# Modulation slices asked for only while the projections' loader has nothing waiting

## The chip, the core and the metric

The kernel runs on one core of one Trainium2 chip. The metric is the device time of one launch in microseconds (us), the median of several runs. TensorE is called PE (its weight loads PEld), VectorE DVE, ScalarE ACT, GpSimd POOL, SyncE SP. SP issues most of the DMAs.

## The reference

Two decoder layers work on x, 1024 tokens by 1024 features in float32. In each layer three vectors, shift, scale and gate, come from the conditioning vector c and modulate the layer's input and output:

```python
mod = c_act @ w_mod + b_mod                    # c_act = silu(c), w_mod: 1024 x 3072 per layer
shift, scale, gate = jnp.split(mod[:, None, :], 3, axis=-1)
h = rms_norm(x, pre_gain) * (1.0 + scale) + shift
proj = h @ w_in                                # 1024 x 3088
...                                            # attention, retention, gated linear attention
y = jnp.concatenate([a_out, r_out, g_out], axis=-1) @ w_out
return x + gate * rms_norm(y, post_gain)
```

Shift and scale are needed before a layer's projections, gate only at its output.

## The kernel before

The program is written out by Python generators. PE's instructions stand in the order in which the generators emit them; the other engines' order is made by a scheduler that starts from that order. The main thread of `layer(l)` goes through the projections: gg and rg (gates), then rq, rk and rv with the retention of eight token tiles, then gqk, gv and kv, then aq0 and aq1, ag0 and ag1, and the output product with w_out. All products are done as three passes over a high and a low part of each operand, so every weight is split when it is loaded.

Beside the main thread run jobs: generators that do one step and yield a delay. A planner's clock, `clk` (in us), advances with an estimated cost for each matmul (`mult`); `pump` runs each job whose due time has passed. The delays stand in the table `L` by name (`lat`), with "@1" for layer 1.

Two kinds of jobs bring in weights, and both use the same five stage buffers, `stage()`, of 128 x 512 floats (tag "st", BST = 5), which other rows use too (the row of post-norm gain, L378).

- The loader of the projections' weights. `request` puts a quarter of a unit (256 KB) into the list `queue` and starts the job `loader` if none runs. `loader` takes an entry, issues its DMA on SP (L152) and appends it to `flying`; when more than LAG + 1 = 3 would be in flight it converts the oldest first (`convert`). A conversion writes the high part (ACT L147 or DVE L149) and the low part (DVE or POOL L535) into the unit's place in the arena, and frees the stage buffer. Between two steps it yields 1.2.
- The modulation, `mod_third(l, j)` with j = 0 for shift, 1 for scale, 2 for gate. For each half of 512 columns it takes eight slices of w_mod, 128 x 512 floats each (256 KB): stage buffer, DMA on SP, and one product-and-sum on DVE into `acc` (L363 for the first, L365 for the others), and yields `mod2`, 4.0. After the eighth it yields `mod3`, and matmuls sum `acc` over its partitions (one of 128 x 512 with a matrix of ones for the gate, four with a single column otherwise). Layer 0's shift and scale are made by another function at the start.

Layer l starts the job for its own gate after its gg and rg projections, and behind it the next layer's scale and shift. There are 64 such slices: 16 each for gate 0, scale 1, shift 1 and gate 1.

Other lines that are spoken of: L163 all matmuls, L178 transposes; in the retention, ACT's L147 copies the transposed q and k out of PSUM, DVE's L1173 masks the scores, L1192 and L1194 renew the running state stR; L963 writes the low part of a gated output, which SP stores to mixS; POOL's L638 is a power for the norms. L147 is thus both a weight's conversion (arena<-st) and a copy out of PSUM (t<-aux, t<-mm).

Of the kernel before, what the change touches and what calls it, by code (L numbers as in the profile page):

```python
# [91 lines left out]
def trunk(ctx: ExitStack, tc: tile.TileContext, ins, cst, out):  # L92
# [24 lines left out]
    def stage():  # L117
        return gp.tile([P, 512], F32, tag="st", name=nm("st"), bufs=BST)
# [7 lines left out]
    def aux(dt=F32):  # L126
        return ps.tile([P, 512], dt, tag="aux", name=nm("aux"), bufs=8 - MMB)
# [23 lines left out]
    def dma(k, dst, src):  # L151
        {"S": nc.sync, "A": A, "P": G}[EN[k]].dma_start(dst, src)  # L152
# [9 lines left out]
    def mult(dst, lhsT, rhs, start, stop, cost=None):  # L162
        T.matmul(dst, lhsT, rhs, start=start, stop=stop)  # L163
        if cost is not None:
            clk[0] += cost
            return
        n = 1
        for d in rhs.shape[1:]:
            n *= d
        c = n / 2400.0  # L170
        if rhs.dtype == F32R:
            c = max(c, 0.107 if lhsT.shape[-1] > 64 else 0.055)
        else:
            c = max(4 * c, 0.21 if n > 2 else 0.03)
        clk[0] += c
# [5 lines left out]
    def lat(key, l):  # L181

        return L[key + "@1"] if l and key + "@1" in L else L[key]

# [3 lines left out]
    def flag(name, lat=0.0):  # L188
        flags[name] = clk[0] + lat
# [73 lines left out]

    modc = {}
    modg = {}

    def mod_rows(l, j, eng=nc.sync):
        rows = t1()[0:16, 0:P]
        eng.dma_start(rows[0:8, :], b_mod[l:l + 1, j * D:(j + 1) * D].rearrange("o (k p) -> (o k) p", p=P))
        eng.dma_start(rows[8:16, :], pre_g[l:l + 1, :].rearrange("o (k p) -> (o k) p", p=P))  # L270
        return rows

    def mod_rows_t(rows, pool=aux):
        pr = pool()
# [68 lines left out]
    def mod_third(l, j):  # L343
        wv = w_mod[l].rearrange("(p k) n -> p k n", k=KT)
        if j < 2:
            mod_tile(l, j)
            rows = mod_rows(l, j)
            yield lat("mod1", l)
            rc = mod_rows_t(rows)
        else:  # L350
            res = cp.tile([P, D], F32, name=nm("modg"), tag="modg")
            modg[l] = res
        for hh in range(2):
            c0 = j * D + 512 * hh
            acc = gp.tile([P, 512], F32, tag="acc", name=nm("acc"), bufs=1)
            if j == 2:
                G.memset(acc, 0.0)
                nc.sync.dma_start(acc[0:1, :], b_mod[l:l + 1, c0:c0 + 512])
            for k in range(KT):
                wt = stage()  # L360
                dma("lwm", wt, wv[:, k, c0:c0 + 512])
                if k == 0 and j < 2:
                    V.tensor_scalar(acc, wt, c_act[:, k:k + 1], None, ALU.mult)  # L363
                else:
                    V.scalar_tensor_tensor(acc, wt, c_act[:, k:k + 1], acc, ALU.mult, ALU.add)  # L365
                yield lat("mod2", l)
            yield lat("mod3", l)
            pm = aux()
            if j < 2:
                for b in range(4):  # L370
                    mult(pm[:, b:b + 1], acc[:, b * P:(b + 1) * P], ones[:, 0:1], True, True)
                mod_cols(l, j, hh, pm, rc)
                if j == 0:
                    flag(("modh", l, hh), lat("mod4", l))
            else:
                mult(pm, allones, acc, True, True)
                gain = stage()
# [87 lines left out]
    def unit(l, name):  # L465
        return place(PLACE[l][name])


    queue, flying = [], []

    def convert():
        conv, st = flying.pop(0)
# [123 lines left out]
    def sw_second():  # L596
        drain()
        for k in range(4):
# [7 lines left out]
            sw_split("T4", k, s4, "t4")  # L606
            yield L["sw1"]
        for name in ("T2", "T3", "T4"):
# [48 lines left out]
    def pre(l, t, xt, early=False, soon=False):  # L657
# [1010 lines left out]

B2, B1, BS, BST, MMB, SMB = 10, 8, 11, 5, 3, 3
EN = {"shw0": "V", "shw1": "A", "shw2": "A", "shw3": "A", "slw0": "V", "slw1": "G", "slw2": "V", "slw3": "G", "sht2": "A", "sht3": "A", "sht4": "A", "slt2": "V", "slt3": "G", "slt4": "G", "sd": "V", "mh0": "A", "mh1": "A", "mh2": "A", "mh3": "A", "mf": "A", "ms0": "V", "ms1": "V", "ms2": "V", "ms3": "V", "yg0": "V", "yg1": "V", "ml0": "V", "ml1": "V", "ml2": "V", "ml3": "V", "mod0": "A", "mod1": "V", "qst": "S", "smh": "S", "sml": "S", "sm0": "S", "sm1": "S", "lao": "S", "sao": "S", "lmix": "S", "ssg": "S", "lsg": "S", "ssr": "S", "lsr": "S", "lx": "S", "sx": "A", "lw": "S", "lwm": "S", "whi0": "V", "whi1": "A", "whi2": "A", "whi3": "A", "wlo0": "V", "wlo1": "V", "wlo2": "V", "wlo3": "G", "xn0": "V", "xn1": "V", "hlo0": "V", "hlo1": "V", "rot0": "V", "rot1": "V", "rdec": "V", "kslo": "V", "qslo": "V", "vlo": "G", "kT": "A", "qT": "A", "sprev": "A", "pn": "G", "pf0": "A", "aoc": "A", "hng": "V", "mh": "A", "gso": "V", "mg": "V", "mgl": "V", "rT": "A", "rv": "A", "gv": "A", "gk": "A", "ak0": "V", "ak1": "V", "ak2": "V", "ak3": "V", "kd0": "G", "kd1": "G", "kd2": "G", "kx1": "G", "kx2": "G", "kx3": "V", "kx4": "V", "qb": "G", "stx": "V"}  # L1670
L = {"sw1": 0.4, "ld1": 1.2, "ld2": 1.2, "ld1@1": 1.2, "ld2@1": 1.27, "swW00": 0.0, "swT1": 0.0, "swW11": 0.4, "swW10": 0.5, "tt1": 8.0, "tt2": 1.75, "tb1": 24.5, "tb2": 0.75, "pf3": 13.2, "pf1": 6.35, "pf2": 4.16, "mod1": 4.6, "mod2": 4.0, "mod3": 13.29, "mod4": 7.04, "mod5": 3.36, "mod6": 9.04, "pre1": 7.44, "kv1": 3.1, "kv2": 2.11, "aq1": 6.0, "aq7": 6.0, "ag1": 5.44, "aq2": 2.4, "aq6": 5.2, "aq3": 10.21, "aq4": 7.36, "aq5": 3.6, "hn1": 8.93, "hn2": 2.85, "gz1": 11.18, "gz2": 8.13, "gl1": 2.76, "gd3": 15.9, "gc1": 0.62, "gc2": 1.94, "gc3": 1.33, "gc4": 0.87, "gc6": 0.86, "gc5": 1.14, "rc1": 0.8, "rc2": 1.09, "rc3": 5.87, "rc4": 2.51, "fin1": 7.28, "lay1": 1.13, "gc4@1": 0.93, "mod2@1": 4.0, "mod3@1": 15.1, "mod5@1": 3.36, "mod6@1": 4.11, "pre1@1": 7.44, "kv1@1": 2.79, "kv2@1": 5.28, "aq1@1": 4.8, "aq7@1": 5.28, "ag1@1": 6.25, "aq2@1": 0.82, "aq6@1": 6.0, "aq3@1": 10.9, "aq4@1": 4.4, "aq5@1": 5.15, "hn1@1": 8.12, "hn2@1": 2.85, "gz1@1": 15.91, "gz2@1": 10.94, "gl1@1": 4.6, "gd3@1": 15.9, "gc1@1": 0.48, "gc2@1": 1.94, "gc3@1": 1.33, "gc6@1": 0.86, "gc5@1": 1.04, "rc1@1": 0.37, "rc2@1": 0.84, "rc3@1": 1.9, "rc4@1": 2.79, "fin1@1": 4.28, "lay1@1": 1.7}
CHUNK = 7
LAG = 2
VDB = 8
# [32 lines left out]
```

## Time and profile before

| | us |
|---|---|
| three runs | 1005.52, 1007.46 (median), 1011.33 |
| the profiled execution | 1010.63 |
| its span in the trace | 1008.9 |
| PE busy | 975.4 |
| DVE busy | 684.5 |
| ACT busy | 408.8 |
| POOL busy | 234.4 |

How to read the rows. In a table by stretch a row has the stretch, its length, then the busy time of PE, PEld, DVE, ACT and POOL with the number of instructions, then the granted clock of PE (1.00 is full), the busy share of the 16 DMA engines and GB/s. In a timeline a row has the start, the time taken, the engine, line, operation, written and read tiles and shapes, how many instructions are merged, and in brackets the idle time before with what ended it; SPq is a DMA's issue, not its transfer. A row of the chain of waits has start, time and what; a DMA there lasts from its issue to its landing. In the DMA list the last figures are the size of one and the median from issue to landing. A row of the waits has total, number of times and the longest.

### The profile page before, as it was taken

How to read it: one execution, taken by the hardware profiler on the slowest of the kernel's cores; microseconds unless marked ns; L12 is line 12 of the kernel's file. 1: busy time of each engine (PE TensorE's matmuls, PEld its weight loads, DVE VectorE, ACT ScalarE, POOL GpSimd, SP SyncE). 2: the span in 40 equal slices, each digit the busy share in tenths (PEclk: the TensorE clock that was granted, in tenths of full speed). 3: DMA queues.
4: the chain of work that ended last, by engine and by line, in shares of the span. 5: the costliest groups of instructions: out<-in, count | busy, mean ns of one | idle time of the engine just before them, and what ended most of it. 6: DMA issues, size and time to landing. Idle time of an engine off the chain costs nothing.

```text
span 1008.9 us, 19610 instructions
## 1 busy us (share of the span) xinstructions
PE 975.4 (97%) x7137; PEld 829.5 (82%) x7137; DVE 684.5 (68%) x1680; ACT 408.8 (41%) x1152; POOL 234.4 (23%) x275
## 2 busy tenths in 40 slices
PE   5899999899999999999999999999999999999897
PEld 1499999888998777778889999998899877777785
DVE  3789857757666778564578275785666577566876
ACT  2476311223322656632465232123332256663321
POOL 2310001223320234330112000113332034544100
PEclk8899999999999999999999999999999999999999
DMA  9942513623326355577655251353132434378883
GB/s 293 308 137 76 173 45 100 170 81 96 96 74 199 89 149 163 171 239 244 214 157 173 64 158 32 108 150 100 41 104 85 125 90 130 112 236 249 265 263 140
DMA packets 129836, 148.73 MB, mean 147 GB/s; under 512 B 14046, under 2 KB 94152, under 8 KB 129740
## 3 DMA queue, kind: packets, MB, share of 16 engines
q1 hardware_dynamic: 124044, 137.92, 45.3%
q10 hardware_dynamic: 5696, 9.56, 2.6%
q8 instruction: 56, 0.92, 0.4%
q14 instruction: 40, 0.33, 0.1%
HBM read 109.17 MB, written 36.18 MB: 144 GB/s over the span
## 4 chain that ended last, share of the span: by engine, by line
PE 80%; DVE 8%; DMA 7%; issue 2%; POOL 1%; ACT 1%; SPq 0%; POOLq 0%; DVEq 0%; ACTq 0%
PE mm L163 61%; PE aux L163 14%; PE aux L178 5%; DMA st<-in_w_in_dram 2%; DMA st<-in_w_out_dram 1%; POOL sm L638 1%; DMA xk<-in_x_dram 1%; DMA wm<-in_w_mod_dram 1%; DMA t<-aoS 1%; DVE arena L535 1%; DMA st<-in_w_mod_dram 1%; DMA t<-sgS 1%; DVE t L328 0%; DVE st L572 0%; DMA mixF<-t 0%
## 5 line engine op out<-in xcount | busy, mean ns | idle before, releaser
L163 PE MATMUL mm<-arena 128*128 128x256 f32 (+2 forms) x1824 | 299.2, 318 | 1.8 <-ACT arena L707 1.8
L163 PE MATMUL mm<-arena,arena 128*128 128x256 f32 (+2 forms) x1824 | 300.7, 318 | 0.0
L163 PEld LDWEIGHTS mm<-arena 128*128 128x128 f32 x1824 | 254.6, 191 | 26.5 <-issue 4.1
L163 PEld LDWEIGHTS mm<-arena,arena 128*128 128x128 f32 x1824 | 254.1, 189 | 25.5 <-issue 4.6
L638 POOL TENSOR_TENSOR sm<-sm,mhalf 128x1 f32<-128x1 f32 (+1 forms) x64 | 56.1, 877 | 347.0 <-DVE sm L637 328.6
L163 PE MATMUL mm<-arena,mx 128*128 128x512 f32 (+1 forms) x564 | 132.4, 392 | 2.9 <-ACT kept L1335 2.9
L163 PEld LDWEIGHTS mm<-arena,mx 128*128 128x128 f32 x564 | 103.1, 191 | 27.1 <-ACT kept L1335 3.3
L147 ACT ACTIVATE t<-aux 128x256 f32<-128x256 f32 (+2 forms) x124 | 55.7, 467 | 76.1 <-PE aux L178 64.8
L147 ACT ACTIVATE arena<-st 128x512 fp32r<-128x512 f32 x94 | 56.1, 626 | 59.1 <-DMA st<-in_w_in_dram 21.4
L535 POOL TENSOR_TENSOR arena<-st,arena 128x512 fp32r<-128x512 f32 x31 | 43.2, 1395 | 138.9 <-ACT arena L147 100.9
L926 POOL TENSOR_TENSOR smx<-smx,sm 128x512 f32<-128x512 f32 x32 | 36.1, 1127 | 124.3 <-DVE sm L925 116.1
L535 DVE TENSOR_TENSOR arena<-st,arena 128x512 fp32r<-128x512 f32 x77 | 59.5, 795 | 6.1 <-ACT arena L147 4.1
L922 ACT ACTIVATE smx<-smx,sm 128x129 f32<-128x129 f32 x128 | 49.9, 392 | 28.4 <-DVE sm L919 28.4
L178 PE MATMUL aux<-c_ident,t 128*128 128x128 f32 (+1 forms) x292 | 48.8, 285 | 7.6 <-DVE t L669 7.2
L365 DVE SCALAR_TENSOR_TENSOR acc<-st,c_act,acc 128x512 f32<-128x512 f32 x60 | 45.5, 759 | 12.6 <-DMA st<-in_w_mod_dram 12.1
L178 PEld LDWEIGHTS aux<-c_ident,t 128*128 128x128 f32 (+1 forms) x292 | 35.4, 145 | 15.2 <-DVE t L669 9.0
L701 ACT ACTIVATE t<-aux,mod,mod 128x128 f32<-128x128 f32 x68 | 25.9, 458 | 43.8 <-DVE t L1242 18.2
L970 ACT ACTIVATE t<-aux 128x256 f32<-128x256 f32 x32 | 12.3, 383 | 75.5 <-PE aux L163 63.4
L163 PEld LDWEIGHTS aux<-t,mx 32*128 32x128 f32 (+1 forms) x896 | 39.5, 187 | 3.8 <-issue 2.1
L163 PE MATMUL aux<-t,mx 32*128 32x32 f32 (+1 forms) x896 | 40.7, 273 | 0.0
L917 DVE COPY_PREDICATED smx<-c_curmask,aux 128x256 f32<-128x256 int32 x64 | 25.5, 447 | 18.8 <-ACT smx L147 15.3
L1242 DVE SCALAR_TENSOR_TENSOR t<-t,sm,t 128x512 f32<-128x512 f32 x32 | 24.0, 779 | 18.6 <-DMA t<-in_x_dram 11.9
(220 smaller groups left out, 1384.3 us busy)
## 6 DMA issues: line engine op xcount, KB each, us to landing
st<-in_w_in_dram SPq DMA_DIRECT2D x96, 256.0 KB, 3.1
st<-in_w_mod_dram SPq DMA_DIRECT2D x64, 256.0 KB, 3.3
st<-in_w_out_dram SPq DMA_DIRECT2D x52, 256.0 KB, 3.8
mx<-mixS SPq DMA_DIRECT2D x20, 512.0 KB, 6.2
mixS<-t SPq DMA_DIRECT2D x72, 128.0 KB, 2.3
wm<-in_w_mod_dram SPq DMA_DIRECT2D x12, 512.0 KB, 8.0
t<-in_x_dram SPq DMA_DIRECT2D x24, 256.0 KB, 4.8
t<-tabS SPq DMA_DIRECT2D x16, 256.0 KB, 3.7
```

The costliest lines, as they stand in the source:

```text
L147: A.activation(dst, src, AF.Copy)
L163: T.matmul(dst, lhsT, rhs, start=start, stop=stop)
L178: T.transpose(dst, src, idn)
L365: V.scalar_tensor_tensor(acc, wt, c_act[:, k:k + 1], acc, ALU.mult, ALU.add)
L535: e.tensor_tensor(lo, st, f(hi), ALU.subtract)
L638: G.tensor_tensor(r, r, mhalf[:, :w], ALU.pow)
L701: A.activation(hf[:, ks], at[kt], AF.Identity, scale=gain, bias=shift)
L917: V.copy_predicated(sv, curmask.unsqueeze(1).to_broadcast((P, 2, P)), pv[:, :, n // P - 1, :])
L922: A.activation(sm[:, h, :], sm[:, h, :], AF.Exp, bias=mx[:, h:h + 1], accum_out=sums[:, h:h + 1])
L926: eng("pn").tensor_tensor(sm[:, :, 0:128], sm[:, :, 0:128], rs.unsqueeze(2).to_broadcast((P, 4, P)), ALU.mult)
L970: A.activation(sq, po, AF.Square)
L1242: V.scalar_tensor_tensor(xt[j], yg[j], r, xt[j], ALU.mult, ALU.add)
```

## The change

Before each slice of the modulation the job now looks whether the loader has anything in `queue` or in `flying`, and as long as it has, yields `mod7`, 1.0, and looks again. The delay after each slice, `mod2`, goes from 4.0 to 2.0 in both layers. The two lists are created earlier in the file, which moves line numbers by one to three. The tests are made while the program is written out, against the planner's clock; the program on the chip contains no such test.

```diff
     modc = {}
     modg = {}
+    queue, flying = [], []
...
             for k in range(KT):
+                while queue or flying:
+                    yield lat("mod7", l)
                 wt = stage()
                 dma("lwm", wt, wv[:, k, c0:c0 + 512])
                 if k == 0 and j < 2:
...
-    queue, flying = [], []
-
     def convert():
...
-L = {... "mod1": 4.6, "mod2": 4.0, ... "mod2@1": 4.0, ...}
+L = {... "mod1": 4.6, "mod7": 1.0, "mod2": 2.0, ... "mod2@1": 2.0, ...}
```

More of the change, by code (lines that the diff above doesn't have):

```diff
@@ L1670 @@
 EN = {"shw0": "V", "shw1": "A", "shw2": "A", "shw3": "A", "slw0": "V", "slw1": "G", "slw2": "V", "slw3": "G", "sht2": "A", "sht3": "A", "sht4": "A", "slt2": "V", "slt3": "G", "slt4": "G", "sd": "V", "mh0": "A", "mh1": "A", "mh2": "A", "mh3": "A", "mf": "A", "ms0": "V", "ms1": "V", "ms2": "V", "ms3": "V", "yg0": "V", "yg1": "V", "ml0": "V", "ml1": "V", "ml2": "V", "ml3": "V", "mod0": "A", "mod1": "V", "qst": "S", "smh": "S", "sml": "S", "sm0": "S", "sm1": "S", "lao": "S", "sao": "S", "lmix": "S", "ssg": "S", "lsg": "S", "ssr": "S", "lsr": "S", "lx": "S", "sx": "A", "lw": "S", "lwm": "S", "whi0": "V", "whi1": "A", "whi2": "A", "whi3": "A", "wlo0": "V", "wlo1": "V", "wlo2": "V", "wlo3": "G", "xn0": "V", "xn1": "V", "hlo0": "V", "hlo1": "V", "rot0": "V", "rot1": "V", "rdec": "V", "kslo": "V", "qslo": "V", "vlo": "G", "kT": "A", "qT": "A", "sprev": "A", "pn": "G", "pf0": "A", "aoc": "A", "hng": "V", "mh": "A", "gso": "V", "mg": "V", "mgl": "V", "rT": "A", "rv": "A", "gv": "A", "gk": "A", "ak0": "V", "ak1": "V", "ak2": "V", "ak3": "V", "kd0": "G", "kd1": "G", "kd2": "G", "kx1": "G", "kx2": "G", "kx3": "V", "kx4": "V", "qb": "G", "stx": "V"}
-L = {"sw1": 0.4, "ld1": 1.2, "ld2": 1.2, "ld1@1": 1.2, "ld2@1": 1.27, "swW00": 0.0, "swT1": 0.0, "swW11": 0.4, "swW10": 0.5, "tt1": 8.0, "tt2": 1.75, "tb1": 24.5, "tb2": 0.75, "pf3": 13.2, "pf1": 6.35, "pf2": 4.16, "mod1": 4.6, "mod2": 4.0, "mod3": 13.29, "mod4": 7.04, "mod5": 3.36, "mod6": 9.04, "pre1": 7.44, "kv1": 3.1, "kv2": 2.11, "aq1": 6.0, "aq7": 6.0, "ag1": 5.44, "aq2": 2.4, "aq6": 5.2, "aq3": 10.21, "aq4": 7.36, "aq5": 3.6, "hn1": 8.93, "hn2": 2.85, "gz1": 11.18, "gz2": 8.13, "gl1": 2.76, "gd3": 15.9, "gc1": 0.62, "gc2": 1.94, "gc3": 1.33, "gc4": 0.87, "gc6": 0.86, "gc5": 1.14, "rc1": 0.8, "rc2": 1.09, "rc3": 5.87, "rc4": 2.51, "fin1": 7.28, "lay1": 1.13, "gc4@1": 0.93, "mod2@1": 4.0, "mod3@1": 15.1, "mod5@1": 3.36, "mod6@1": 4.11, "pre1@1": 7.44, "kv1@1": 2.79, "kv2@1": 5.28, "aq1@1": 4.8, "aq7@1": 5.28, "ag1@1": 6.25, "aq2@1": 0.82, "aq6@1": 6.0, "aq3@1": 10.9, "aq4@1": 4.4, "aq5@1": 5.15, "hn1@1": 8.12, "hn2@1": 2.85, "gz1@1": 15.91, "gz2@1": 10.94, "gl1@1": 4.6, "gd3@1": 15.9, "gc1@1": 0.48, "gc2@1": 1.94, "gc3@1": 1.33, "gc6@1": 0.86, "gc5@1": 1.04, "rc1@1": 0.37, "rc2@1": 0.84, "rc3@1": 1.9, "rc4@1": 2.79, "fin1@1": 4.28, "lay1@1": 1.7}
@@ new lines @@
+L = {"sw1": 0.4, "ld1": 1.2, "ld2": 1.2, "ld1@1": 1.2, "ld2@1": 1.27, "swW00": 0.0, "swT1": 0.0, "swW11": 0.4, "swW10": 0.5, "tt1": 8.0, "tt2": 1.75, "tb1": 24.5, "tb2": 0.75, "pf3": 13.2, "pf1": 6.35, "pf2": 4.16, "mod1": 4.6, "mod7": 1.0, "mod2": 2.0, "mod3": 13.29, "mod4": 7.04, "mod5": 3.36, "mod6": 9.04, "pre1": 7.44, "kv1": 3.1, "kv2": 2.11, "aq1": 6.0, "aq7": 6.0, "ag1": 5.44, "aq2": 2.4, "aq6": 5.2, "aq3": 10.21, "aq4": 7.36, "aq5": 3.6, "hn1": 8.93, "hn2": 2.85, "gz1": 11.18, "gz2": 8.13, "gl1": 2.76, "gd3": 15.9, "gc1": 0.62, "gc2": 1.94, "gc3": 1.33, "gc4": 0.87, "gc6": 0.86, "gc5": 1.14, "rc1": 0.8, "rc2": 1.09, "rc3": 5.87, "rc4": 2.51, "fin1": 7.28, "lay1": 1.13, "gc4@1": 0.93, "mod2@1": 2.0, "mod3@1": 15.1, "mod5@1": 3.36, "mod6@1": 4.11, "pre1@1": 7.44, "kv1@1": 2.79, "kv2@1": 5.28, "aq1@1": 4.8, "aq7@1": 5.28, "ag1@1": 6.25, "aq2@1": 0.82, "aq6@1": 6.0, "aq3@1": 10.9, "aq4@1": 4.4, "aq5@1": 5.15, "hn1@1": 8.12, "hn2@1": 2.85, "gz1@1": 15.91, "gz2@1": 10.94, "gl1@1": 4.6, "gd3@1": 15.9, "gc1@1": 0.48, "gc2@1": 1.94, "gc3@1": 1.33, "gc6@1": 0.86, "gc5@1": 1.04, "rc1@1": 0.37, "rc2@1": 0.84, "rc3@1": 1.9, "rc4@1": 2.79, "fin1@1": 4.28, "lay1@1": 1.7}
```

## The prediction, made before the changed kernel ran

> **What bounds the kernel now.** I read the engine shares first, then a table of busy time by stretch, then the PE timeline in the stretches that are not full, and last the queue of each engine that PE waited for there. Lines are those of the kernel before.
>
> ```profile
> span 1008.9 us, 19610 instructions
> PE 975.4 (97%) x7137; PEld 829.5 (82%) x7137; DVE 684.5 (68%) x1680; ACT 408.8 (41%) x1152; POOL 234.4 (23%) x275
> ...
> 150.00:175.00 25.00, 24.46 (x203) 23.25 (x203) 16.78 (x51) 3.50 (x8) 2.96 (x3) 1.00 0.35 98
> 175.00:200.00 25.00, 21.91 (x176) 20.73 (x176) 19.06 (x51) 8.51 (x17) 6.66 (x5) 0.98 0.57 160
> 200.00:225.00 25.00, 25.00 (x141) 21.69 (x140) 13.88 (x35) 5.60 (x13) 6.98 (x10) 0.89 0.26 77
> 225.00:675.00 450.00, 449.39 (x3410) 390.32 (x3410) 304.50 (x762) 184.51 (x535) 99.87 (x119) 1.00 0.47 142
> 675.00:690.00 15.00, 12.34 (x75) 10.21 (x75) 7.27 (x19) 4.08 (x9) 3.30 (x3) 1.00 0.64 185
> 690.00:900.00 210.00, 209.88 (x1747) 172.50 (x1746) 138.25 (x354) 99.57 (x323) 70.56 (x84) 1.00 0.37 110
> ```
>
> PE is the bound: its first figure nearly equals the length of the stretch. The change moves no work into the start or the last 100 us, so between 150 and 900 us only PE's idle time can be won: 0.54 + 3.09 + 0 + 0.61 + 2.66 + 0.12 = 7.0 us, and what the granted clock of 0.98 and 0.89 (the figure before the last two) costs. Where it is lost:
>
> ```profile
> 172.48 0.71 PE L163 MATMUL aux<-t 64*128 64x128 f32 x6 [0.54 <-DVE t L963]
> ...
> 194.43 2.11 PE L163 MATMUL mm<-arena,arena 128*128 128x512 f32 x8
> 199.62 1.23 PE L163 MATMUL aux<-t 64*128 64x128 f32 x8 [3.09 <-ACT t L147]
> 200.78 3.78 PE L163 MATMUL mm<-arena,arena 128*128 128x512 f32 x8
> ...
> 209.60 0.38 PE L163 MATMUL aux<-stR,t 128*128 128x128 f32 x2
> ```
>
> ```profile
> 195.50:198.90 3.40, 1.04 (x5) 0.51 (x3) 0.35 (x1) 0.71 (x2) 0.01 (x1) 1.00 0.86 252
> 198.90:202.30 3.40, 2.67 (x12) 2.17 (x13) 1.18 (x3) 0.67 (x2) 1.25 (x1) 0.50 0.80 229
> 202.30:205.70 3.40, 3.40 (x13) 2.92 (x12) 0.00 (x0) 0.00 (x0) 0.00 (x0) 0.50 0.37 120
> ...
> 678.00:681.40 3.40, 2.12 (x21) 1.82 (x20) 1.43 (x3) 1.11 (x2) 0.00 (x0) 1.00 0.96 318
> ```
>
> The 3.09 us stall costs more than itself: the 3.4 us around it hold 1.04 us of matmul (31%), and the next 6.8 us run at clock 0.50. A stretch with 2.12 of 3.40 (62%) kept 1.00. I call 195 to 210 us place A and 675 to 690 us place B. Both are the last tiles of a layer's retention stage, where layer 0's or 1's weight slices gqk, gv and kv come through the five stage buffers.
>
> ```profile
> 192.08 0.63 ACT L147 ACTIVATE arena<-st 128x512 fp32r<-128x512 f32 x1 [1.23 <-DMA st<-in_w_in_dram]
> 194.41 0.63 ACT L147 ACTIVATE arena<-st 128x512 fp32r<-128x512 f32 x1 [1.70 <-DMA st<-in_w_in_dram]
> 194.95 0.36 ACT L147 ACTIVATE t<-mm 128x256 f32<-128x256 f32 x1
> 198.19 0.63 ACT L147 ACTIVATE arena<-st 128x512 fp32r<-128x512 f32 x1 [2.87 <-DMA st<-in_w_in_dram]
> ```
>
> ```profile
> 186.84 4.86 SPq L152 DMA_DIRECT2D st<-in_w_in_dram  x3
> 191.80 0.41 SPq L152 DMA_DIRECT2D mixS<-t  x1
> 192.30 0.38 SPq L152 DMA_DIRECT2D st<-in_w_in_dram  x1
> ...
> 194.00 2.20 SPq L152 DMA_DIRECT2D st<-in_w_mod_dram  x3
> ```
>
> ```profile
> 165.96 5.29 DMA st<-in_w_mod_dram
> ...
> 192.30 5.80 DMA st<-in_w_in_dram
> ```
>
> These are ACT's row, SP's issues and two pieces of the chain of waits. ACT takes its list in order. The conversion of kv's last slice sits at 198.19, because that slice, asked for at 192.30, needed 5.80 us; the copy that PE needs stands behind it. At 172.48 it is a slice of the modulation that blocks: asked for at 165.96, 5.29 us.
>
> **The change part by part.** The counts on every engine are the same in both programs (6197 PE, 1682 DVE, 1004 ACT, 280 POOL, 638 SP); it moves instructions only. Each slice moved is one DMA on SP and one product on DVE; the sum over bias and gain, one matmul per half of the gate, moves with it. Compared in program order, the conversions of the projection weights keep their places within some 50 matmuls; what changes is which load stands in front of which.
>
> *At 172.* The sixth slice of the gate's second half, which blocked DVE there, is now asked for before gqk's loads instead of between them:
>
> ```profile
> 171.34 0.75 DVE L365 SCALAR_TENSOR_TENSOR acc<-st,c_act,acc 128x512 f32<-128x512 f32 x1 [3.83 <-DMA st<-in_w_mod_dram]
> ```
>
> The eight products still stand ahead of the same L963, but no load of theirs is now asked for behind a load of gqk. Gain 0.54 (bounds 0 and 0.54).
>
> *Place A.* Order of requests before: gqk, slice, gqk, gqk, gv, slice, gv, gv, slice, gv, kv x4, gain row, slices. After: all slices of the gate, gqk x4, gv x3, gain row, gv, kv x4, slices. The buffers then free like this:
>
> ```profile
> 187.66 1.29 POOL L535 TENSOR_TENSOR arena<-st,arena 128x512 fp32r<-128x512 f32 x1
> ...
> 190.62 1.89 DVE L535 TENSOR_TENSOR arena<-st,arena 128x512 fp32r<-128x512 f32 x3
> ```
>
> kv's first load now takes the buffer of gv's last slice (free at 187.66 + 1.29 = 188.95, 2.1 later than now), the others those freed by the three products of 0.63 each, the first of them moved ahead of one instruction (L1151): 190.6, 191.6, 192.2. So kv's last load is asked for at 192.2, as before; only the store of mixS at 191.80 no longer stands before it, and no row of gain right behind it. What it takes from there is the open term. The page's median for such a load is 3.1 us, this one took 5.80:
>
> ```profile
> st<-in_w_in_dram SPq DMA_DIRECT2D x96, 256.0 KB, 3.1
> st<-in_w_mod_dram SPq DMA_DIRECT2D x64, 256.0 KB, 3.3
> ```
>
> Three loads stand within 1.6 us ahead of it, so I take 4.0: landing at 196.2 (bounds 195.3 and 198.0). From the landing (198.10) to PE's start (199.62) are now 1.5; one copy more (0.36, the row at 194.95) stands between, so PE starts again at 198.1. PE itself runs out at 194.43 + 2.11 = 196.54, and the gate's product is moved in front of that:
>
> ```profile
> L163 PE MATMUL aux<-acc,c_ones x8: 591/592/593, 153.5 to 702.3; 128*128 128x512 f32 x8
> ```
>
> so 197.1. The stall is 1.0 instead of 3.09; the 3.4 us around it hold 2.4 us of matmul (70%, above the 62% that kept the clock), so the half clock goes. From 199.62 to 209.60 PE now needs 9.98, of which 6.08 at half clock; without it 6.94. *What is late next:* eight slices now follow kv in a row, 2 units of the planner's clock apart instead of 4, and three of their products stand on DVE right before the update of stR, for which PE waits at 209.60. Behind the store that follows ACT's copy, they are asked for at about 198.8, 199.2 and 199.6; 3.3 us to land and 0.75 of product give 204.4, and stR is renewed 1.3 us later, at 205.7. PE would be there at 198.1 + 6.94 = 205.0, so it waits 0.7 and stands at that matmul at 205.7 instead of 209.60. With the 0.59 of the moved product, which falls away later, the gain is 4.5. Bounds: 0, if the load takes 5.8 again, and 3.09 + 3.04 = 6.1 with no stall and no half clock. [...]
>
> *Place B.* The same, without the clock:
>
> ```profile
> 680.77 0.72 PE L163 MATMUL aux<-t 64*128 64x128 f32 x8 [1.28 <-ACT t L147]
> 681.41 3.04 PE L163 MATMUL mm<-arena 128*128 128x512 f32 x12
> 685.46 0.46 PE L163 MATMUL aux<-stR,t 128*128 128x128 f32 x2 [1.01 <-DVE stR L1194]
> ```
>
> ```profile
> 679.60 0.63 ACT L147 ACTIVATE arena<-st 128x512 fp32r<-128x512 f32 x1 [3.77 <-DMA st<-in_w_in_dram]
> 680.14 0.58 ACT L147 ACTIVATE t<-aux 128x512 f32<-128x512 f32 x1
> 681.71 1.40 ACT L147 ACTIVATE arena<-st 128x512 fp32r<-128x512 f32 x2 [0.99 <-DMA st<-in_w_in_dram]
> ```
>
> kv's loads are asked for 5 us (first) to 1 us (last) earlier, since two slices no longer stand in between. But in the changed order ACT has two more conversions, those of kv's last two slices, in front of the copy at 680.14; they wait for landings that now come at 681.71 and, two conversions in 1.40 us, about 682.5. 1 us earlier, the last is converted at 682.1, the copy done at 682.7 and PE's matmul of 680.77 comes 2 us later. Behind it 1.01 of wait, 0.4 of a second one and the product moved ahead (0.59) fall away. I take 0; bounds a gain of 2.66 (all idle time there) and a loss of 5.4 (the slow rival below).
>
> *Elsewhere.* Between 270 and 285 three slices go through one buffer one after another, and DVE waits for them, up to 2 us by an estimate from their 3.3 us to land. PE covers it: in the 450 us from 225 on it idled 0.61 us, though DVE waited in the same manner there (nine waits of all, 12.1 us):
>
> ```profile
> DVE acc L365 <- DMA st<-in_w_mod_dram: 12.1, 9, 3.8
> ```
>
> 0 taken, 1 us lost if that cover fails. The added waiting step issues nothing on any engine, it only delays the planner's job; nothing hangs on it but the sums of gate, gain and shift, which layer 1 needs from 525 us on and which stand no later in the new order than in the old.
>
> **Sum.** -0.5 - 4.5 + 0 = -5.0 us against the profiled execution, which took 1010.63 (span 1008.9 and 1.73 around it). The median of the three runs, 1007.46, is 3.2 lower, and the runs spread by 5.8; a stall that sets off the half clock in one run and not in the next would spread them so. So I count 4.0 of the 5.0 for the median: **1003.5 us**.
>
> **Rivals.** *The load stays late* (A unchanged, kv's last load 5.8 us again): landing 198.0, PE at 199.9, stall 2.8, half clock stays; -0.5 in all, 1007. For it: kv's last load is asked for no earlier. Against: fewer transfers around it. [...]
>
> *Slower: place B becomes what A was.* If kv's last load lands there at 682.5 as now, since the row of gain is asked for ahead of three of kv's loads instead of behind them, the copy behind it is done at 683.7 and PE's matmul comes at 683.8 instead of 680.77. 3.7 us later (0.65 + 3.04) PE is at 687.5 instead of 685.46: 2.0 lost. PE has then been idle for over 3 us in a row, as at A, and the half clock follows: 6.8 us at 0.50, 3.4 lost. 5.4 in all; with A unchanged but for the 0.7 wait, -0.5 + 0.7 + 5.4 = +5.6: 1013. It decides from a landing at 682 on, where the idle time reaches 3 us. For it: conversions ahead of the copy are what stalls A. Against: in front of it PE also waits for a mask that now stands behind kv's second slice, which parts the idle time in two, and 62% kept the clock.
>
> *Both places clear:* kv lands after 3.1 us, the slices are in time, B loses its idle time: -0.5 - 5.6 (A's 6.1 less 0.5 for the products) - 2.7 = -8.8, 999. For it: fewer transfers stand before kv in both places.
>
> *The change doesn't do what it says:* "nothing waiting" is the planner's list, not the chip's queue. The new order does keep all slices out of the gqk, gv, kv loads in both layers; so only a small chance, 1007.5.
>
> **Chances.** Forecast 0.38 (its own range 1000.5 to 1006.5), late load 0.22, place B slower 0.20, both clear 0.15, nothing 0.05. A measurement of this kernel tells about 0.5% (5 us) from no change: faster is below 1002.4, slower above 1012.5. Faster: two fifths of the forecast (0.15) and both clear, 0.30. Slower: most of the slow rival and an edge of the late load, 0.18. Same: 0.52. Range 999 to 1013: below it lies half of "both clear", above it half of the slow rival, 0.18 together; it takes in the bounds of A and of B singly.
>
> **What would show it.** Right: no slice between the loads of 176 to 192 us, the wait before the matmul of 199.62 at about 1 us, clock 1.00 throughout 195 to 210, the stR matmul near 206, B's idle time still 2 to 3 us. Wrong: kv's last landing at 198 again; a wait of over 2 us for DVE L1194 at A; clock 0.50 anywhere between 150 and 900, at B above all; idle time in 225 to 675.

## The result, and the profile after

The changed kernel takes 1015.27 us (median of 11 runs, 1010.41 to 1018.61), the kernel before on the same chip 1005.5 us (11 runs, 1001.91 to 1011.33): a ratio of 1.009, 95% interval 1.0064 to 1.0116. It is slower by 9 to 10 us, where 4 us less were forecast. In a later batch of runs it was 1012.01 against 1004.54 us, 1.0077 (1.0057 to 1.0097). The profiled execution took 1015.75 us, with a span of 1014.0.

The same table by stretch as for before (length, busy PE, PEld, DVE, ACT and POOL with counts, granted clock, DMA share, GB/s), now of the changed kernel. Its lines stand one to three below those of before: L368 is the product (before L365), L1174 the mask of the scores, L1193 and L1195 renew the state stR, L381 asks for the row of gain.

```profile
150.00:175.00 25.00, 25.00 (x218) 24.46 (x217) 21.08 (x61) 5.27 (x12) 3.88 (x3) 1.00 0.48 131
175.00:200.00 25.00, 25.00 (x185) 22.47 (x184) 18.00 (x46) 7.68 (x17) 4.68 (x4) 1.00 0.60 183
200.00:225.00 25.00, 22.85 (x207) 19.55 (x207) 16.52 (x44) 7.29 (x19) 7.10 (x10) 0.93 0.34 99
225.00:675.00 450.00, 446.81 (x3294) 388.44 (x3291) 301.87 (x748) 179.38 (x526) 102.18 (x119) 0.99 0.45 138
675.00:690.00 15.00, 12.41 (x63) 9.59 (x63) 7.34 (x16) 2.92 (x6) 3.18 (x3) 0.77 0.64 188
690.00:900.00 210.00, 208.53 (x1736) 172.47 (x1735) 136.19 (x348) 95.69 (x310) 66.80 (x81) 1.00 0.34 102
```

PE's idle time between 150 and 900 us has grown from 7.0 to 9.4 us (0 + 0 + 2.15 + 3.19 + 2.59 + 1.47), and the clock is now low in three stretches, one of them at place B (0.77). What the change was to take away at 172 and 199 us is gone: the first two rows are full.

**Place A.** The first fence has PE's timeline there, the second DVE's, the third SP's issues, the fourth one piece of the chain of waits.

```profile
193.46 0.71 PE L163 MATMUL aux<-t 64*128 64x128 f32 x8
...
196.84 3.98 PE L163 MATMUL mm<-arena,arena 128*128 128x512 f32 x16
202.96 0.46 PE L163 MATMUL aux<-stR,t 128*128 128x128 f32 x2 [2.15 <-DVE sm L638]
```

```profile
198.40 0.75 DVE L368 SCALAR_TENSOR_TENSOR acc<-st,c_act,acc 128x512 f32<-128x512 f32 x1 [2.50 <-DMA st<-in_w_mod_dram]
200.00 1.54 DVE L368 SCALAR_TENSOR_TENSOR acc<-st,c_act,acc 128x512 f32<-128x512 f32 x2 [0.85 <-DMA st<-in_w_mod_dram]
201.46 0.58 DVE L1193 TENSOR_TENSOR stR<-stR,aux 64x128 f32<-64x128 f32 x2
...
202.40 0.41 DVE L1195 TENSOR_TENSOR stR<-stR,c_cdt 128x256 f32<-128x256 f32 x1
```

```profile
193.77 5.73 SPq L152 DMA_DIRECT2D st<-in_w_mod_dram  x6
```

```profile
194.30 5.61 DMA st<-in_w_mod_dram
```

The scores (aux<-t, 64x128) start at 193.46 without a wait: kv's last conversion no longer holds up ACT. But the next product with stR waits 2.15 us. Its release is put down to L638, a step of 0.16 us; the update L1195, just before it on DVE, is what the matmul reads. In front of the update stand three products of scale's first half, waiting for slices of which one took 5.61 us from issue to landing. The stall was handed on, not removed.

**Place B.** PE, ACT, DVE and SP of the changed kernel:

```profile
679.28 0.38 PE L163 MATMUL aux<-stR,t 128*128 128x128 f32 x2
682.25 1.11 PE L163 MATMUL aux<-t,t 128*128 128x64 f32 x4 [2.59 <-DVE t L1174]
```

```profile
680.50 0.63 ACT L147 ACTIVATE arena<-st 128x512 fp32r<-128x512 f32 x1 [5.60 <-DMA st<-in_w_in_dram]
```

```profile
681.16 0.69 DVE L536 TENSOR_TENSOR arena<-st,arena 128x512 fp32r<-128x512 f32 x1 [4.28 <-ACT arena L147]
681.77 0.75 DVE L1174 TENSOR_TENSOR t<-aux,c_causal 128x256 f32<-128x256 f32 x2
```

```profile
675.82 0.34 SPq L381 DMA_DIRECT2D st<-in_post_norm_gain_dram  x1
676.28 0.37 SPq L152 DMA_DIRECT2D st<-in_w_in_dram  x1
```

Read from below: kv's second load is asked for at 676.28, behind the row of gain. ACT is idle for 5.60 us until that load has landed and converts at 680.50, DVE makes the low part at 681.16, and the mask of the scores stands behind that on DVE. PE waits for the mask.

**Layer 0's gated linear attention** (GLA below), PE and then DVE:

```profile
259.03 1.54 PE L163 MATMUL aux<-t,mx 32*128 32x32 f32 x48
...
261.65 0.33 PE L178 MATMUL aux<-c_ident,t 128*128 128x128 f32 x1 [0.48 <-DVE mx L1116]
```

```profile
260.03 0.75 DVE L368 SCALAR_TENSOR_TENSOR acc<-st,c_act,acc 128x512 f32<-128x512 f32 x1
260.69 0.69 DVE L1081 TENSOR_TENSOR t<-t,t 128x512 f32<-128x512 f32 x1
261.29 0.90 DVE L1116 COPY_PREDICATED mx<-c_mask,aux 128x128 f32<-128x128 int32 x4
```

A product of scale's second half now stands on DVE shortly ahead of the masked copies L1116, and PE waits 0.48 us. (That the product is the cause did not hold, see gate0_only below.) The wait is little, but look at the clock. Stretches of the same trace, cut where the granted clock changes:

```profile
200.80:204.21 3.41, 1.26 (x13) 1.28 (x12) 2.70 (x7) 0.00 (x0) 1.24 (x1) 1.00 0.79 244
204.21:207.63 3.42, 3.42 (x11) 2.75 (x11) 2.58 (x6) 0.38 (x1) 0.95 (x3) 0.50 0.56 143
258.83:262.24 3.41, 2.93 (x66) 2.48 (x65) 3.41 (x14) 2.49 (x9) 0.00 (x0) 1.00 0.43 106
262.24:272.48 10.24, 10.24 (x90) 9.95 (x90) 5.60 (x18) 1.36 (x7) 2.98 (x6) 0.50 0.65 195
...
678.67:682.08 3.41, 0.99 (x6) 0.66 (x4) 0.92 (x2) 0.90 (x2) 0.00 (x0) 1.00 0.98 313
682.08:688.90 6.82, 6.66 (x25) 4.92 (x26) 3.88 (x11) 2.02 (x4) 2.38 (x2) 0.50 0.71 213
```

Each half clock follows a window of 3.41 us: 1.26 of 3.41 busy at A, 0.99 at B, but 2.93 (86%) in the GLA.

**Where the time went.** Matching the same matmuls in two traces gives how much later PE is at each place. All against the second trace of before, which shows no half clock from 150 to 900 us; that execution, 1001.93 us, was the fastest of its twelve, so the lags are larger than against a run in the middle. The lag at 100 us, which differs from run to run, is subtracted (us):

| trace | 199 | 220 | 262 | 270 | 320 | 440 | 660 | 690 | 900 |
|---|---|---|---|---|---|---|---|---|---|
| before, first | 2.6 | 3.6 | 3.9 | 3.9 | 3.9 | 3.9 | 3.9 | 4.8 | 4.6 |
| after, first | -3.4 | 1.0 | 2.5 | 6.2 | 6.9 | 8.7 | 8.6 | 13.6 | 13.8 |
| after, second | -3.0 | 0.9 | 1.8 | 1.4 | 2.3 | 4.5 | 4.4 | 8.2 | 9.4 |
| gate1_as_before | -3.0 | -0.6 | 0.6 | 3.0 | 3.7 | 5.2 | 5.1 | 6.5 | 6.6 |
| sum_late | -2.0 | -2.0 | -2.0 | -1.4 | 0.6 | 1.7 | 1.6 | 3.9 | 4.0 |
| mended | -1.9 | -1.9 | -1.7 | -1.7 | -1.2 | -2.0 | 0.6 | 2.7 | 2.7 |

After is ahead by 3 us at 199 and has given all of it back by 220, wait and half clock together. Against the first trace of before, from which the forecast was made, it is still 2.6 us ahead at 220 (1.0 against 3.6). Then it loses 3.7 in the GLA (in one of two traces), about 2 between 320 and 440, and 3.8 to 5.0 at B.

### The profile page after: what moved, and what is told of

The parts are those of the page before. It is cut to its first block, busy times and chain, and to the rows that moved or that the text cites. A ratio compares the mean times of both kernels' runs of the same rounds, so it can differ in the third digit from the quotient of the medians.

```text
span 1014.0 us, 19621 instructions
## 1 busy us (share of the span) xinstructions
PE 980.2 (97%) x7137; PEld 833.8 (82%) x7137; DVE 689.9 (68%) x1680; ACT 407.2 (40%) x1152; POOL 236.2 (23%) x275
## 4 chain that ended last, share of the span: by engine, by line
PE 78%; DMA 9%; DVE 7%; issue 2%; ACT 1%; POOL 1%; SPq 1%; ACTq 0%; POOLq 0%; DVEq 0%
PE mm L163 59%; PE aux L163 14%; PE aux L178 4%; DMA wm<-in_w_mod_dram 1%; DMA xk<-in_x_dram 1%; DMA st<-in_w_out_dram 1%; DMA t<-xs 1%; POOL sm L639 1%; DMA st<-in_w_in_dram 1%; DMA out_dram<-t 1%; DMA t<-mixF 1%; DVE t L1243 1%; DMA st<-in_w_mod_dram 1%; DMA t<-aoS 1%; SPq L152 1%
## 5 line engine op out<-in xcount | busy, mean ns | idle before, releaser
L163 PEld LDWEIGHTS mm<-arena,arena 128*128 128x128 f32 x1824 | 257.0, 191 | 25.1 <-issue 3.5
L927 POOL TENSOR_TENSOR smx<-smx,sm 128x512 f32<-128x512 f32 x32 | 38.3, 1198 | 141.5 <-DVE sm L926 118.0
L368 DVE SCALAR_TENSOR_TENSOR acc<-st,c_act,acc 128x512 f32<-128x512 f32 x60 | 46.2, 770 | 7.0 <-DMA st<-in_w_mod_dram 6.5
L163 PEld LDWEIGHTS aux<-kT,mx 64*128 64x128 f32 x384 | 24.6, 186 | 10.9 <-issue 6.7
```

The lines of the kernel that those rows point to most:

```text
L927: eng("pn").tensor_tensor(sm[:, :, 0:128], sm[:, :, 0:128], rs.unsqueeze(2).to_broadcast((P, 4, P)), ALU.mult)
```

## The experiments

Twelve kernels, each timed beside before on the same chip. Working theory, **three places**: the loss is made of the wait and half clock at B, the half clock in the GLA and short waits, while A is really won. It fell at A, as gate0_only shows, and its reading of the GLA fell there too.

**The two kernels again.** No edit.

> The kernel before once more, for a second trace and the granted clocks of its runs. Theory 'three places' (the loss is a longer wait of PE at 675 to 690 us with a half clock behind it, a half clock of 10 us in layer 0's gated linear attention, and short waits at 400 to 450; the wait at 199 us is really gone): about 1005.5, and half clock in the middle of the span only near 199 us. Rival 'chance' (the half clock falls where it likes, and the two traces merely caught different falls): a half clock somewhere else in the middle, at 262 or 682 us as well, or none at 199 us.

> The changed kernel once more. Three places: about 1015, with a wait of over 2 us before the transposes near 682 us again and a half clock behind it; the half clock near 262 us comes back in at least part of the runs. Chance: the half clocks lie elsewhere and the time is nearer to 1010.

Measured: before 1004.46 us, a ratio to itself of 1.0002 (0.9986 to 1.0019); after 1.0077 (1.0057 to 1.0097). The second trace of before, at place A: PE's wait, and the two windows of the trace's clock grid that it falls in.

```profile
196.91 0.71 PE L163 MATMUL aux<-t 64*128 64x128 f32 x8 [3.11 <-ACT t L147]
```

```profile
192.28:195.70 3.42, 1.52 (x7) 0.90 (x5) 0.82 (x2) 0.40 (x2) 0.00 (x0) 1.00 0.75 201
195.70:199.11 3.41, 2.20 (x15) 1.81 (x16) 1.18 (x3) 1.15 (x3) 1.26 (x1) 1.00 0.86 293
```

The wait is the same (3.11, in the first trace 3.09), but no half clock follows. It is cut by a window's edge at 195.70, so that neither window is as empty as the one of the first trace (1.04 of 3.40). "Chance" is right on this point: the same stall costs a half clock in one run and none in the next. Three places is right on the waits: the second trace of after has 1.66 us before stR and 2.82 at B, again with half clocks behind both (204.64 to 208.05 and 679.09 to 682.51), but none in layer 0's GLA (one of 3.4 us in layer 1's, from 726.88).

**Undoing it piece by piece.** gate1_as_before:

```diff
-                while queue or flying:
+                while (queue or flying) and (l, j) != (1, 2):
...
-                yield lat("mod2", l)
+                yield 4.0 if (l, j) == (1, 2) else lat("mod2", l)
```

> Gate 1 goes without the test and at the old delay of 4.0; all else as in the changed kernel. Three places: the wait and half clock near 682 us fall back to the 2.66 us of idle time of before, about 4.5 us less than the changed kernel: 1010.5, a ratio to before of 1.005. Rival 'bunching' (slices close together load DVE and the DMA queues and the loss is spread over layer 0): no gain from this, 1014 to 1015. Chance: no fixed relation.

Measured: 1007.42 us, 1.0039 (1.0021 to 1.0057). B has 2.95 us of idle time, about the old 2.66, and no half clock:

```profile
675.00:690.00 15.00, 12.05 (x72) 9.90 (x72) 6.96 (x19) 3.75 (x9) 3.30 (x3) 1.00 0.62 183
```

So gate 1 makes up about half of the loss: 4.6 us of 7.5 by the medians of the one batch, at B and in layer 1's GLA behind it (the half clock at 726.88 in the second trace of after is not in this one either). Bunching is out for that half. B is not always free of a half clock with gate 1 as before: of seven such traces, those of gate0_only, sum_late, mended and small_burst have one of 3.4 us there, those of before, before_again and gate1_as_before none.

gate0_only keeps test and 2.0 for (l, j) == (0, 2) alone:

```diff
-                while queue or flying:
+                while (queue or flying) and (l, j) == (0, 2):
...
-                yield lat("mod2", l)
+                yield lat("mod2", l) if (l, j) == (0, 2) else 4.0
```

> Test and delay 2.0 for gate 0 alone; scale and shift of layer 1 without the test at 4.0, gate 1 as before. Three places: the gain at 172 and 199 us is kept and nothing of the rest: 3 to 5 us under before, 1000.5 to 1002.5, a ratio of 0.996. Bunching: the same sign, since the slices behind gate 0 go at the old pace. A gain at 199 us that is not there (rival 'nothing was won'): 1005.5, a ratio of 1.000.

Measured: 1008.59 us (1000.82 to 1010.85), 1.003 (1.0008 to 1.0051). It should have shown the gain at A by itself, and is slower than before. In its trace PE waits 2.66 us before the matmul with stR at 205.18, and half clocks follow there (3.4 us), at 263.76 (10.2 us) and, at B, at 683.60 (3.4 us). Here my theory fell: A is not won. It is not the delay of scale's slices that puts three of their products ahead of the update of stR, for here it is the old 4.0 and they stand there all the same, at 201.43. What is left is that scale starts earlier. My new theory, **products in front**: gate 0 ends earlier, its sum frees the gate's accumulator `acc`, of which there is one, earlier, and the scheduler then takes the products of scale as soon as DVE has nothing else ready, ahead of the update of stR.

The same trace speaks against my reading of the GLA. PE there in gate0_only, then in the first trace of before:

```profile
262.08 0.44 PE L178 MATMUL aux<-c_ident,t 128*128 128x128 f32 x2
263.17 0.33 PE L178 MATMUL aux<-c_ident,t 128*128 128x128 f32 x1 [0.66 <-DVE mx L1116]
263.26 2.10 PE L163 MATMUL mm<-arena,arena 128*128 128x256 f32 x10
```

```profile
265.51 1.08 PE L163 MATMUL mm<-arena,arena 128*128 128x256 f32 x7
266.88 0.33 PE L178 MATMUL aux<-c_ident,t 128*128 128x128 f32 x1 [0.28 <-DVE mx L1115]
```

gate0_only has no product of scale on DVE between 208.0 and 281.1 us, and PE waits 0.66 us and the half clock comes all the same. What differs is PE's own order: before has seven matmuls of 128x256 (1.08 us) in front of the transpose that waits, gate0_only none. In the six traces without the seven (both of after, gate1_as_before, gate0_only, gain_late, fill_b) the wait is 0.48 to 0.66 us; in seven traces with them (both of before, sum_late, mended, gate1_free, before_gate1, small_burst) it is at most 0.28. PE's order is that of the generators, so the moved jobs have shifted the main thread's matmuls too. Which moved step of the planner's clock does it was not tested.

The earlier start of scale was tried next, by holding back the sums that free `acc`. sum_late is gate1_as_before with

```diff
-            yield lat("mod3", l)
+            yield lat("mod3", l) + (8.0 if (l, j, hh) == (0, 2, 1) else 0.0)
```

> As gate1_as_before, and the sum over gate 0's second half held back by 8 more, so that its accumulator comes free later and the products of scale's first half stand behind the update of stR on DVE instead of in front of it. Theory 'products in front' (the wait at 199 us was not removed but handed on to the matmul with stR at 203, 1.65 us and a half clock in part of the runs): that wait falls under 0.5 us, 2 to 3 us less than gate1_as_before's 1007.4: 1005. Rival 'landing' (the wait at 203 comes from something else, such as the transfers themselves): the wait stays over 1.5 us and the time at 1007.

and mended adds 20.0 for (l, j, hh) == (1, 1, 0) in the same line.

> As sum_late, and the sum over the first half of scale held back by 20 more, so that the products of its second half stand behind the scores of the gated linear attention. Three places: no wait over 1 us and no half clock between 150 and 670 us, 2 to 3 us less than sum_late by the half clock near 262 in part of the runs: 1002 to 1003, a ratio to before of 0.998. Bunching: no difference from sum_late.

Measured: sum_late 1005.34 us, 1.0021 (1.0000 to 1.0042); mended 1003.86 us, 0.9997 (0.9982 to 1.0011). PE in sum_late at A:

```profile
194.74 0.71 PE L163 MATMUL aux<-t 64*128 64x128 f32 x8 [1.31 <-ACT t L147]
...
201.84 0.38 PE L163 MATMUL aux<-stR,t 128*128 128x128 f32 x2
```

The wait before stR is gone, as "products in front" says: on DVE the update L1193 stands at 199.57 and the first product of scale at 202.84, though two of its slices were asked for at 195.02. Since the edit holds back the whole job with the sum, it shows that scale's early start does the harm; that it does so through `acc` is argued, not shown. 1.31 us are back at the copy behind kv. PE's seven matmuls in the GLA are back in their place, and the wait there is 0.14. And mended, by stretch:

```profile
150.00:225.00 75.00, 73.58 (x634) 67.33 (x632) 55.38 (x151) 19.89 (x47) 16.76 (x19) 1.00 0.47 138
225.00:470.00 245.00, 244.47 (x1820) 199.15 (x1817) 167.66 (x397) 106.05 (x339) 70.94 (x88) 1.00 0.48 146
```

1.4 us of idle time at A, 0.5 from there to 470, the clock at 1.00: GLA and 320 to 440 are clean. What mended takes away in layer 0 beside sum_late is a wait of 1.62 us at 291.34 and one of 0.53 at 279.81; near 262 sum_late's trace had no half clock left. The runs of mended spread by 5.6 us (1000.95 to 1006.57), those of gate0_only by 10.0. The three steps 1.0077, 1.0039, 1.0021, 0.9997 take the whole loss away; neighbouring intervals touch or overlap, that of gate1_as_before and that of mended do not. Nothing is gained over before: by the table mended keeps 2.0 us as far as 440 and loses 2.6 to 660 (a wait of 1.51 at 497.52) and 2.1 at B in this trace (2.79 of wait and a half clock of 3.4 from 679.28).

**Which half of the change.** pace2_nowait has the delay 2.0 without the test.

```diff
-                while queue or flying:
-                    yield lat("mod7", l)
```

> The delay of 2.0 alone, without the test on the loader. Theory 'products in front': the wait near 199 us comes back, since slices stand between kv's loads again, and the half clock near 262 comes in part of the runs, since scale's second half still stands in the gated linear attention; at 682 the row of gain and the slices all stand well in front of kv, so the wait there is not above the 2.66 us of before: 1006 to 1009. Rival 'test' (the loss is the test's alone): 1004.5 as before.

Measured: 1009.53 us (1004.0 to 1018.26), 1.0052 (1.0027 to 1.0077). The wait at 199 us is 1.44 + 0.44 us rather than 3, a new one of 1.42 at 219.66 is followed by a half clock of 10.2 us from 222.14, one of 1.62 at 266.24 by another of 3.4; from 660 to 690 us it has no wait at all. So the test is not the sole cause, and in this trace the place B is best off, with the slices well ahead of gqk.

**What holds up kv at B.** gain_late: the row of gain of gate 1 waits as the slices do.

```diff
+                while l == 1 and (queue or flying):
+                    yield lat("mod7", l)
                 gain = stage()
```

> The changed kernel, and the row of gain of gate 1 also held until the loader is done, so that it does not stand between kv's first and second load and takes none of the five buffers from them. Theory 'row of gain' (the wait at 679 to 682 us is kv's second load, which comes late for that row): the wait falls from 2.6-2.8 to under 1.5 us, and the kernel is 2 to 4 us faster than the changed one, 1008.5 to 1010.5. Rival 'all slices in front' (gqk's loads start later because eight slices stand ahead of them, and so does everything behind): no change, 1012.

Measured: 1010.72 us (1003.97 to 1014.09), 1.0059 (1.0036 to 1.0082). PE at B:

```profile
674.17 0.77 PE L163 MATMUL aux<-t,t 128*128 128x64 f32 x4 [0.84 <-DVE t L1176]
...
678.30 0.71 PE L163 MATMUL aux<-t 64*128 64x128 f32 x8 [1.33 <-ACT t L147]
```

The wait for the mask falls from 2.59 and 2.82 to 0.84, 1.33 comes back at the copy, and no half clock follows. The row of gain is thus a part of what makes kv's second load late; in the median the gain over the changed kernel (1.0059 against 1.0077) is within the intervals.

gate1_free and before_gate1 let gate 1 run ahead instead, at 2.0 and without the test. gate1_free is mended with the delay of gate 1 at 2.0 in place of 4.0; against the changed kernel that is the line below and the held-back sums of mended. before_gate1 is before with the second edit alone.

```diff
-                while queue or flying:
+                while (queue or flying) and (l, j) != (1, 2):
```

```diff
-                yield lat("mod2", l)
+                yield 2.0 if (l, j) == (1, 2) else lat("mod2", l)
```

> As mended, but gate 1 goes at the delay 2.0 without the test, in place of the old 4.0: its slices and its row of gain stand ahead of gqk's second load, and kv's four loads follow one another. Theory 'place' (what is left of the time between mended and a clean 675 to 690 us is the wait there, 2.8 us in mended's trace and none in that of the delay alone): no wait over 0.6 us at 670 to 690, 2 to 4 us under mended: 1000 to 1002, a ratio to before of 0.996 to 0.998. Rival 'traces differ by chance': as mended, 1.000.

> The kernel before, with gate 1 alone at the delay 2.0, without any test: its last slices and its row of gain stand ahead of gqk's loads, and kv's loads follow one another; layer 0 is as before. Theory 'place' (the idle time at 675 to 690 us, 1.9 us in the second trace of before and 2.66 in the first, hangs on what stands between kv's loads): none over 0.6 us there, about 2 us under before, 1002 to 1003, a ratio of 0.998; half of it may be given back at 716 and 737, where gate1_free and the delay alone wait 0.53 and 0.67 us. Rival 'all slices in front': the wait stays, 1.000 or above.

Measured: 1004.4 us, 1.0000 (0.9983 to 1.0017), where 1000 to 1002 were expected, and, where 1002 to 1003 were, 1007.24 us (1001.25 to 1011.37), 1.0011 (0.9989 to 1.0033). Place B of gate1_free:

```profile
670.00:690.00 20.00, 19.89 (x128) 17.47 (x127) 9.87 (x24) 5.95 (x16) 6.82 (x9) 1.00 0.41 121
```

B can be emptied of waits, as "place" said; its time did not follow, and is still that of before. In before_gate1 the gain is given back behind: a wait of 0.67 us at 741.04 in layer 1's GLA, and

```profile
737.66:741.07 3.41, 2.74 (x65) 2.30 (x64) 3.41 (x14) 2.63 (x11) 0.00 (x0) 1.00 0.13 42
741.07:751.31 10.24, 10.24 (x89) 9.95 (x90) 3.54 (x16) 2.08 (x9) 2.48 (x6) 0.50 0.25 81
```

the same 10.24 us of half clock as in layer 0's GLA. By the matching of matmuls this trace loses 5.1 us from 692 to 752, 1.2 of it in two waits (0.53 and 0.67), so about 4 by the clock. No version here beats before by more than its interval.

**What the half clock follows.** fill_b adds work where PE waits at B in the changed kernel:

```diff
         po = aux()
+        if (l, t) == (1, 6):
+            fw = unit(l, "gqk")
+            for _ in range(6):
+                mult(po.rearrange("p (s n) -> p s n", s=2), fw[:, 0, 0, 0:P], fw[:, 0, 0:2, 0:256], True, True, 0.0)
```

> The changed kernel, with six more matmuls of 128x512 (1.6 us by the rows of that shape) on PE in layer 1 where it waits at 679 to 682 us for the mask; their result is overwritten, so they add work and change no output. Theory 'streaming' (the granted clock falls for at least 3.41 us when in a window of 3.41 us, on a grid fixed for the run, PE streams less than about a quarter of what it could): the end of the wait stays, no half clock follows it at 679 to 689, and the kernel is 1.7 to 3.4 us faster than the changed one, 1009 to 1010. Rival 'wait' (the clock falls for having waited, whatever else PE does in the window): half clock stays, same time or up to 1.6 us slower, 1012 to 1014.

```profile
674.49 1.54 PE L163 MATMUL aux<-arena 128*128 128x512 f32 x6
675.88 0.38 PE L163 MATMUL aux<-stR,t 128*128 128x128 f32 x2
677.65 0.77 PE L163 MATMUL aux<-t,t 128*128 128x64 f32 x4 [1.39 <-DVE t L1174]
```

```profile
680.26:690.00 9.74, 9.54 (x53) 7.82 (x53) 4.85 (x14) 1.25 (x5) 2.79 (x3) 1.00 0.33 94
```

The wait ends where it would, the clock stays at 1.00, and PE loses 2.7 us from 660 to 690 instead of 3.8 to 5.0. But the median, 1012.94 us (6 runs), 1.0093 (1.0068 to 1.0118), does not show it: inconclusive as to time. The trace alone shows little too: PE is busy for 2.61 us of the 3.41 from 676.85, and a window of 2.20 kept the clock in before_again while one of 2.93 was followed by half clock in after.

small_burst is before with more small matmuls:

```diff
-            for s in range(1, 4):
+            for s in [1, 2, 3] + ([1, 2, 3] * 12 if (l, p, c) == (0, 1, 0) else []):
```

> The kernel before, with the first 12 of the 32x32 score matmuls of one tile pair in layer 0's gated linear attention (near 265 us) written out twelve times more: 144 small matmuls, 4.6 us at the 1.54 us for 48 of their row, which write the same values again. PE is never idle in them. Theory 'streaming': a window of 3.41 us full of them streams about a tenth of what PE could, so the clock falls for 3.41 or 6.83 us at that place in every trace, and the kernel is 6.3 to 8 us slower than before: a ratio of 1.0063 to 1.008. Rival 'wait': no half clock there, 4.6 us slower, 1.0046.

```profile
239.09 14.16 PE L163 MATMUL aux<-t,mx 32*128 32x32 f32 x336
```

```profile
240.11:243.52 3.41, 3.41 (x132) 3.41 (x128) 0.00 (x0) 0.09 (x1) 0.00 (x0) 1.00 0.31 82
243.52:257.18 13.66, 13.65 (x205) 12.70 (x202) 2.13 (x7) 1.88 (x7) 0.00 (x0) 0.50 0.10 31
```

PE is busy for every bit of the window from 240.11, and the clock is halved for the next 13.66 us. "Wait" is refuted, as far as the profile's busy time goes, in which the ends of matmuls are modelled. The cost, 1017.83 us, 1.0124 (1.0094 to 1.0155), is above both expectations, because I counted the added work wrongly: each of these products is two records, so 288 more, not 144, 9.2 us at 1.54 for 48 (and the pair begins at 239, not 265). The other 3 us of about 12.5 are put down to the clock: the row of 336 took 14.16 us, where 1.54 for 48 make 10.8.

## Why the prediction was wrong

What failed by most are the two zeros of the sum, B and elsewhere: from 220 to 900 us after loses 12.8 and 8.5 us in its two traces, before 1.0 in its first against its second. The 4.5 of A came in part.

- *At 172:* right as a step, the wait is gone. But the second trace of before does not have it either, so it was not there to be won in every run.
- *Place A,* gain 4.5: the first half was right and better than said. Kv's last load is asked for at 187.07, 2.3 us earlier than before once the 2.9 us are taken off by which this trace of after is ahead at 100 us, where the forecast had it as before; it takes 3.66 us (4.0 forecast), and PE waits 0 and 0.32 us at the copy instead of 1.0. **The step that failed here is "what is late next",** and with it "the half clock goes": 0.7 us of wait before stR was forecast, 2.15 and 1.66 came, and a half clock of 3.4 us behind each. With the same 2.9 us put on, the update of stR ends at 205.7 as forecast, and PE is there at 203.7 (196.84 + 3.98 + 2.9) instead of 205.0. That the matmul with stR stands nearly where it was put is thus partly luck: PE came earlier and waited longer. The gate's product that moved ahead is two records, 1.12 us at 188.59, not the 0.59 taken; since it falls away later, it cancels. The forecast counted 3.3 us to land for the slices in front of the update; this trace has one of 5.61. Against the first trace of before, 172 and A together won 2.6 us of the 5.0; against the second, which pays the 3.11 us of wait without a half clock, they lost 1.0.
- *Place B,* 0: **the step that failed is the zero.** After loses 5.0 and 3.8 us there, before 0.9 in its first trace against its second. The rival "place B becomes what A was" had the size, 5.4, and the half clock, but another path: it has PE wait at the copy behind kv's last load, and PE waited for the mask of the scores behind kv's second. My argument against it, that the mask parts the idle time in two, was the mistake: the second load was late, so both waits became one of 2.59 and 2.82 us. That the row of gain stood in front of kv's loads was named in the rival and not weighed in the forecast.
- *Elsewhere,* 0: **the cover that this zero rested on failed,** with 3.19 us of PE idle from 225 to 675 where before had 0.61. I watched DVE's waits for three slices between 270 and 285 and asked whether PE could cover them. I did not ask what the moved jobs do to PE's own order, and took "it moves instructions only" as harmless: the seven matmuls that covered the masked copies in the GLA stood elsewhere, PE waited 0.48 us, and in one trace of two 10.24 us of half clock followed. Waits of 0.93 and 1.34 us for POOL's L927 followed at 428 and 432; there too before has other matmuls in front of the transposes that wait (3.05 us of them against 2.12, and a sum of 1.05 us in front of the second). "Stand no later than in the old order" was true of the sums, and beside the point: they stood earlier.
- *The clock:* "31% of work halves it, 62% keeps it" was the wrong measure. Half clock followed windows of 86% (after, from 258.83) and 100% (small_burst, from 240.11); none followed those of 44% and 65% in before_again (1.52 from 192.28 and 2.20 from 195.70).
- *The base:* 1010.63, the profiled execution, was among the slowest of before. Of the 8.8 us between the spans of the two traces of before, 1.9 lie before 100 us and 2.3 behind 935 (a half clock at 946.40), where nothing was to be won; the forecast took the distance to the median for a sign of the half clock at A.

The lag of 0.9 to 1.5 us that after gathers between 220 and 262 us is for 0.95 the sum of scale's first half, which PE makes at 254.11 here and at 300.2 in before, and for the rest the wait in the GLA. What stays open: why mended waits 1.51 us at 497.52, which step of the planner moves the seven matmuls, and whether `acc` or the earlier place in the job's list puts scale's products in front.

## What to carry to other kernels

A change that makes one job finish earlier moves every job behind it; look up what ties them together, here a single accumulator and a planner's clock, and read where the instructions of the next job, and of the main thread, now stand on each engine, PE too, before you count the gain. A stall taken away is worth only the distance to the next thing that is late, and if you know what that is, compute its time from its own loads and not from the old arrival of the engine. And take a trace of before twice: a half clock can stand in one and not in the other, as behind the waits of 3.09 and 3.11 us at A.

## What the runs showed of the hardware that was not expected

The edges of the granted clock in after lie on one grid of 3.413 us: 204.21, 207.63, 262.24, 272.48, 682.08 and 688.90 are 0, 1, 17, 20, 140 and 142 steps apart. PE's busy time in a window of 3.41 us did not tell whether half clock follows (all these windows ran at 1.00):

| window | PE busy, us | matmuls | what followed |
|---|---|---|---|
| after, from 678.67 | 0.99 | 6 | 6.82 us at 0.50 |
| after, from 200.80 | 1.26 | 13 | 3.42 us at 0.50 |
| before_again, from 192.28 | 1.52 | 7 | 1.00 |
| before_again, from 195.70 | 2.20 | 15 | 1.00 |
| fill_b, from 676.85 | 2.61 | 16 | 1.00 |
| before_gate1, from 737.66 | 2.74 | 65 | 10.24 us at 0.50 |
| after, from 258.83 | 2.93 | 66 | 10.24 us at 0.50 |
| small_burst, from 240.11 | 3.41 | 132 | 13.66 us at 0.50 |

A window without any idle time was followed by half clock too, the one of small_burst. What parts the rows was not shown. That it is how much PE streams in the window ("streaming"), and a quarter as the limit, was the author's estimate: in small_burst the half clock came without a wait as it forecast, for 13.66 us where 3.41 or 6.83 were forecast, and fill_b leaves it open. In the second trace of after PE waits as long among the same matmuls (0.49 us), and the clock stays at 1.00 from 258.4 to 272.0. Where the half clock came in a GLA, a short wait stood right in front of it, 0.48 us in after at 261.65 and 0.67 in before_gate1 at 741.04, and by the matching of matmuls PE lost about 4 us: 3.7 from 262 to 270 in after, about 4 of the 5.1 in before_gate1.
